# Toeplitz tables from TensorE transposes instead of a store and reload, in an S5 diffusion layer

## The chip, the cores and the metric

One core of a Trainium2 chip runs the kernel. The metric is the device time of one execution in microseconds (us), the median of several runs. Engines: PE (TensorE), DVE (VectorE), ACT (ScalarE), POOL (GpSimd), SP (SyncE, which here issues every DMA).

## The reference, cut to what matters

One layer over 256 latent tokens with 256 context tokens, width 2048. The token mixer is an S5 state space with 128 groups of 16 channels and 64 complex states, in two directions. Then come a gated linear unit (GLU) and a squared-ReLU MLP of width 8192, all in float32.

```python
def s5_scan(u, lam_bar, b_bar, s0, reverse):
    bu = jnp.einsum('btgh,gph->btgp', u, b_bar)
    ...
    _, states = lax.associative_scan(_lin_rec_combine, (a, bu), axis=1, reverse=reverse)
    return states
...
    y_lat = u_lat * d
    for direction in range(2):
        ...
        st_ctx = s5_scan(uc_ctx, lam_bar, b_bar, s0, reverse)
        s_ctx_final = st_ctx[:, 0] if reverse else st_ctx[:, -1]
        st_lat = s5_scan(uc_lat, lam_bar, b_bar, s_ctx_final, reverse)
        y_lat = y_lat + jnp.einsum('btgp,ghp->btgh', st_lat, c_mat).real
    ...
        z = jax.nn.gelu(y.reshape(h.shape).astype(h.dtype))
        a, g = jnp.split(z @ w_glu, 2, axis=-1)
        return a * jax.nn.sigmoid(g)
```

`h_lat` is `x` after an RMS norm, a scale and a shift that come from `silu(c) @ w_mod`. The MLP is `jnp.square(jax.nn.relu(h @ w1)) @ w2`.

## The kernel before, in words

**Chunks.** The 256 tokens of a stream are 32 chunks of 8 (`L`). Within a chunk the state space is a fixed linear map from 8x16 inputs to 8x16 outputs per group (a block Toeplitz table with the skip `d` on its diagonal); between chunks only the state is carried. The 128 groups are 16 blocks of 8 (`NB`), and the blocks make three scan units of 4, 6 and 6 (`UNITS`).

**Work of a block b**, each half `hf` being four groups:

1. `xn_blk` and `u_blk` (L565 to L576) normalise and modulate the inputs in place, three operations of 512 columns. POOL does them, but for the modulation of the first two blocks, which is DVE's.
2. `e_sums` (L590, POOL) makes sums of the powers `Qr`, `Qi` and of the matrices `B`. `e_op` (L604, DVE) makes the table `e` with five operations of 512 columns for each half.
3. `e_tr` (L619, PE) transposes `e`, `e_ev` (ACT) copies it out as `et`, `v_mm` (L697, PE) multiplies it with the inputs, and `v_ev` (ACT) puts the results into the unit's scan arrays `ctx` and `lat`.
4. `strip` (L631, PE) multiplies `e` with the block-diagonal matrix `cbd` of `C`, which `c_diag` (ACT) fills. That gives the first block column of the Toeplitz table for both directions. `strip_ev` (ACT) copies it to `sk`. For each pair of blocks `b2`, `w_tr` (L645, PE) transposes it, `w_ev` (ACT) lays it out as one strip `W` of 15 shifts, `dd_mul` (POOL) makes the skip and `w_diag` (L671, DVE) adds it.
5. `w_out` (L676, SP) stores the strip in DRAM, and `load_it` (L685, SP) reads it back with eight DMAs of 128 KB, each at another shift, so that the table `it` stands in SBUF with its rows in place. `it` has one buffer; for the pairs 5 and 7 a second one in another pool.

**Scan of a unit** (`step_op`, L719, DVE): five doubling levels over the context chunks, then 31 steps over the latent chunks of three dependent operations each.

**Output of a block.** `d_sums` (L746, POOL) and `d_op` (L759, DVE, six operations of 512 columns) make the table of `C` times powers, in the ring `dx` of four half-block buffers. `sp_copy` (ACT) and `sp_sum` (L782, POOL) lay out the states. `out_mm` (L785, PE) sums `it` times the inputs and three products of table and states; `gelu` (ACT) and `z_tr` (L806, DVE, a transpose in 32x32 blocks) follow for each pair.

**Weights** come as items of 1 MB in the ring `raw` of three buffers (`RAWBUFS`), in the order in which they are used: 32 of `w_mod` for the scale and shift of the mixer (`a_mm`, L467), 32 for the gates (`k_mm`, L478), and the GLU's. The first ten GLU items are multiplied as they are (`g_mm`, L991), as soon as the gelu outputs that they need exist; the other 22 are split into two parts first (`w_hi`, `w_lo`, then three products at L998) and wait until the whole S5 stage is closed (`close_s5`). After the GLU come the second norm and the MLP (L1325 and L1358), whose loops are written out after the plan.

**The order** of all this is made by `Plan` (L47): a list scheduler that takes each task with its engine, a length in us written in the code, its priority, the tasks before it and the buffers (rings) that it takes and gives back. It emits the tasks in that order, so each engine's queue, and SP's with its DMAs, is a fixed sequence. A task that waits holds up all that stands behind it on its engine. An instruction of POOL or DVE is recorded under L122 where the helper `tt` issued it.

Of the kernel before, what the change touches and what calls it, by code (L numbers as in the profile page):

```python
# [8 lines left out]
F32 = mybir.dt.float32  # L9
# [18 lines left out]
RAWBUFS = 3  # L28
# [11 lines left out]
UNITS = (4, 6, 6)  # L40
PI = math.pi
# [75 lines left out]
def _body(ctx, tc, nc, I, O):  # L117
# [111 lines left out]
    with psx:  # L229
# [15 lines left out]
        m16 = sb.tile([64, H], F32, name="m16")  # L245
        dcol = sb.tile([64, 32], F32, name="dcol")
# [34 lines left out]
        for dst, src in ((m16, "m16"), (dcol, "dcol"), (bcol, "bcol"), (sel4, "sel4")):  # L281
            S.dma_start(dst, I[src])
        V.memset(cst, 0.0)
        V.memset(epst, EPS)
        sk = ew.tile([128, L, 4, H], F32, name="sk")
        cbd = [ew.tile([128, 8, 2, 32], F32, name=f"cbd{n}") for n in range(2)]
        for t in cbd:
            GP.memset(t, 0.0)
# [42 lines left out]
        cm = {V: tmp("c0", [128, NB, 4, 8]), GP: tmp("c1", [128, NB, 4, 8])}  # L331
# [31 lines left out]
        cmul(GP, at(p_, 2), at(p_, 0), at(p_, 1))  # L363
        cmul(GP, span(p_, 4, 8), span(p_, 0, 4), rept(p_, 3, 4))
# [38 lines left out]
        for name, cap in (("ada", 1), ("ev", 1), ("bcb", 2), ("bcs", 2), ("bcc", 2), ("s1e", 2), ("s2e", 1), ("sd", 2), ("cbd", 2),  # L403
                          ("k1", 1), ("dd", 1), ("e", 2), ("et", 2), ("tr", 2), ("st", 1), ("v", 1), ("x", 2), ("yv", 1), ("sk", 1), ("W", 1), ("it", 1),
                          ("ctx", 1), ("lat", 2), ("dx", 4), ("sp", 2), ("z", 1), ("t", 1), ("it2", 1)):
            plan.ring(name, [0.0] * cap)
        plan.ring("raw", [])
        for n in "bsc":
            plan.rings["bc" + n][1].clear()
# [4 lines left out]
        PR = dict(ada=4, T=20, st=3, V=1, W=5, om=5, E=0, D=2, D0=8, gate=0, k4=5, gap=1, p=-1, ars=3, g=6, g2=20, evm=10, eg1=6, x1=6, zlo=4, z=8, ada2=0, k4l=4, acc=20, lo=1, hi=5, sums='Pool', spsum='Pool')  # L414
# [26 lines left out]
        def close_pre():  # L441
            nonlocal lp_, wk, drp
# [3 lines left out]
            drp = p1.enter_context(tc.tile_pool(name="drp", bufs=1, space=bass.MemoryType.DRAM))  # L446

        lp_ = wk = drp = None
        qt = [add("ACT", 0.85, lambda d=d, s=s, l=l: q_copy(d, s, l, 2, NB), prio=1) for d, s in ((Qr, qr), (Qi, qi)) for l in (True, False)]
        pt = [add("ACT", 0.95, lambda d=d, s=s, g=g, l=l: p_copy(d, s, g, l), prio=PR["p"]) for d, s, g in ((Pr, pr, 1.0), (Pn, pi, -1.0)) for l in (True, False)]  # L450
        t = []
# [10 lines left out]
        for n in range(RB, min(nq + RB, len(items))):  # L462
            rawt[n] = add("SP", 2.91, lambda n=n: load_to(n + 1), prio=2, take=("raw",), lag=1.3)
# [74 lines left out]
        for n, key in enumerate(queue):  # L538
# [26 lines left out]
        def xn_blk(b):  # L565
            x = xv[b // BQ][:, :, (b % BQ) * 8:(b % BQ) * 8 + 8]
            tt(GP, x, x, rs.rearrange("p (i c) -> p i c", i=2).unsqueeze(2).to_broadcast([128, 2, 8, C]), ALU.mult)
# [10 lines left out]
        for b in range(NB):  # L578
            t = add("Pool", 1.23, lambda b=b: xn_blk(b), prio=3 + b, ready=28.7)
            on_v = b < 2  # L580
            ut[b] = add("DVE" if on_v else "Pool", 1.33 if on_v else 2.05, lambda b=b, e=V if on_v else GP: u_blk(b, e), [t, vect[chunk_of[b]]],
                        prio=0 if on_v else 2 + b)
# [3 lines left out]
        for b in range(2, NB):  # L586
            for n in "bsc":
                bcl[n, b] = add("SP", 0.45, lambda n=n, b=b: load_bc(n, b), prio=0, take=("bc" + n,), lag=2.0)

        def e_sums(b):  # L590
            Bv = bct.pop(("b", b))
            s1 = ew.tile([128, L, 8], F32, tag="s1e", bufs=2, name="s1e")
# [3 lines left out]
            tt(SE, s2[:, 1], Bv[:, 0], Bv[:, 1], ALU.subtract)  # L596
            est[b] = Bv, s1, s2

        def c_diag(b):
            Cv = bct.pop(("s", b))  # L600
            act(cbd[b % 2][0:64, :, :, 0:H], Cv[0:64].rearrange("p r g h -> p g r h"))
            act(cbd[b % 2][64:128, :, :, H:], Cv[64:128].rearrange("p r g h -> p g r h"))

        def e_op(b, hf, k):  # L604

# [3 lines left out]
            if k == 0:  # L609
                est[b, hf] = (ew.tile([128, 4, L, H], F32, tag="k1e", bufs=1, name="k1"),  # L610
                              ew.tile([128, 2, 4, L, H], F32, tag="e", bufs=2, name="e"))
            k1, e = est[b, hf]
            if k < 3:
                o, p, c = ((k1, s1, Bv[:, 0]), (e[:, 1], Qr[:, b], s2[:, 0]), (e[:, 0], Qi[:, b], s2[:, 1]))[k]
                tt(V, o, p[:, :, hs].rearrange("p t g -> p g t").unsqueeze(3).to_broadcast(n), c[:, hs].unsqueeze(2).to_broadcast(n), ALU.mult)
            else:
                tt(V, e[:, k - 3], k1, e[:, k - 3], ALU.subtract)

        def e_tr(b, hf, r):  # L619
            e = est[b, hf][1]  # L620
            est["ps"] = pst("tr", 2)
            for gi in range(4):
                PE.transpose(est["ps"][:, gi * 128:(gi + 1) * 128], e[:, r, gi].rearrange("p s h -> p (s h)"), ident)  # L623
# [6 lines left out]

        def strip(b, hf):  # L631
            e = est[b, hf][1]
            est["st", b, hf] = st = pst("st", 1)
            for r in range(2):
                for j in range(4):
                    PE.matmul(st[32 * j:32 * j + 32, :128], cbd[b % 2][:, hf * 4 + j, r], e[:, r, j].rearrange("p s h -> p (s h)"),
                              start=(r == 0), stop=(r == 1))

        def strip_ev(b, hf):
            lp = 2 * (b % 2) + hf  # L640
            act(sk[:, :, lp], est.pop(("st", b, hf))[:, :128].rearrange("p (s h) -> p s h", h=H))
# [839 lines left out]
```

## Time and profile before

| what | us |
|---|---|
| median of 3 runs (1309.31 to 1315.62) | 1313.72 |
| the profiled execution's own time | 1313.43 |
| its span, first to last instruction | 1311.7 |
| PE busy | 1178.7 |
| DVE busy | 897.1 |
| ACT busy | 539.4 |
| POOL busy | 192.5 |

The span is 1.7 us short of the execution's time, which is 0.3 us below the median. Busy time is the union of an engine's recorded instructions; for PE their ends are modelled. In the rows further on, a line of the timeline or of a group of instructions reads: start, duration, engine, line, operation, output<-inputs, shape, count; groups give the busy time and the mean in ns of one, then the idle time before them.

### The profile page before, as it was taken

How to read it: one execution, taken by the hardware profiler on the slowest of the kernel's cores; microseconds unless marked ns; L12 is line 12 of the kernel's file. 1: busy time of each engine (PE TensorE's matmuls, PEld its weight loads, DVE VectorE, ACT ScalarE, POOL GpSimd, SP SyncE). 2: the span in 40 equal slices, each digit the busy share in tenths (PEclk: the TensorE clock that was granted, in tenths of full speed). 3: DMA queues.
4: the chain of work that ended last, by engine and by line, in shares of the span. 5: the costliest groups of instructions: out<-in, count | busy, mean ns of one | idle time of the engine just before them, and what ended most of it. 6: DMA issues, size and time to landing. Idle time of an engine off the chain costs nothing.

```text
span 1311.7 us, 22524 instructions
## 1 busy us (share of the span) xinstructions
PE 1178.7 (90%) x9457; PEld 957.2 (73%) x9457; DVE 897.1 (68%) x1200; ACT 539.4 (41%) x731; POOL 192.5 (15%) x200
## 2 busy tenths in 40 slices
PE   4576884696898999989999999999999999999997
PEld 1454553452434688989999999999978888888885
DVE  8999999878878677765555565555655555655555
ACT  5442544242115534574333334333434444444443
POOL 4766344611322000030000000000000000000000
PEclk8588997798899999999999999999999999999998
DMA  7488868989986888816656666566656555555552
GB/s 269 148 213 295 316 245 195 307 307 196 260 227 168 319 346 324 317 66 224 234 219 245 217 220 250 209 242 223 230 189 224 192 193 184 182 185 188 192 192 97
DMA packets 74093, 296.68 MB, mean 226 GB/s; under 512 B 7164, under 2 KB 30588, under 8 KB 48520
## 3 DMA queue, kind: packets, MB, share of 16 engines
q1 hardware_dynamic: 73992, 295.25, 66.3%
q8 instruction: 74, 1.21, 0.4%
q14 instruction: 27, 0.22, 0.1%
HBM read 291.15 MB, written 4.07 MB: 225 GB/s over the span
## 4 chain that ended last, share of the span: by engine, by line
PE 74%; DMA 9%; DVE 5%; SPq 1%; ACT 1%; issue 1%; POOL 0%; DVEq 0%; POOLq 0%; ACTq 0%
PE m L1325 27%; PE o L1358 27%; PE gb L998 9%; DMA raw<-wk 4%; PE gb L991 3%; DMA it<-wd 2%; DMA raw<-wa 2%; DVE e L122 2%; SPq L689 1%; PE ada L484 1%; PE y L800 1%; PE v L706 1%; DMA bcc<-bc 1%; PE m L1247 1%; PE ada L476 1%
## 5 line engine op out<-in xcount | busy, mean ns | idle before, releaser
L122 DVE TENSOR_TENSOR wlo<-raw,whi 128x2048 fp32r<-128x2048 f32 x126 | 288.7, 2291 | 134.7 <-ACT whi L125 134.7
L1325 PE MATMUL m<-h,whi 128*128 128x256 f32 x1984 | 248.2, 283 | 0.0
L125 ACT ACTIVATE whi<-raw 128x2048 fp32r<-128x2048 f32 (+1 forms) x130 | 243.8, 1876 | 1.5 <-PE m L1247 1.5
L1325 PEld LDWEIGHTS m<-h,whi 128*128 128x128 f32 x1984 | 242.5, 192 | 0.0
L1358 PE MATMUL o<-wlo,hh 128*128 128x512 f32 x512 | 160.5, 395 | 0.2 <-DVE wlo L122 0.2
L1358 PE MATMUL o<-whi,hh 128*128 128x512 f32 x512 | 160.6, 395 | 0.0
L1358 PE MATMUL o<-whi,hl 128*128 128x512 f32 x512 | 160.5, 395 | 0.0
L1325 PE MATMUL m<-h,wlo 128*128 128x256 f32 x992 | 129.1, 283 | 0.0
L1325 PEld LDWEIGHTS m<-h,wlo 128*128 128x128 f32 x992 | 123.5, 192 | 0.0
L125 ACT ACTIVATE hh<-hid 128x512 fp32r<-128x512 f32 x64 | 40.5, 633 | 194.5 <-PE o L1358 194.5
L125 ACT ACTIVATE r<-m 128x256 f32<-128x256 f32 x64 | 24.6, 384 | 222.9 <-PE m L1325 221.1
L1358 PEld LDWEIGHTS o<-wlo,hh 128*128 128x128 f32 x512 | 95.9, 187 | 24.1 <-DVE wlo L122 0.6
L1358 PEld LDWEIGHTS o<-whi,hh 128*128 128x128 f32 x512 | 95.8, 187 | 24.2 <-ACT hh L125 0.8
L1358 PEld LDWEIGHTS o<-whi,hl 128*128 128x128 f32 x512 | 96.0, 187 | 23.5
L1297 DVE TENSOR_TENSOR hl<-hid,hh 128x512 fp32r<-128x512 f32 x64 | 44.3, 693 | 88.8 <-ACT hh L125 88.7
L1269 DVE TENSOR_TENSOR hid<-r,m 128x256 f32<-128x256 f32 x64 | 26.9, 421 | 91.9 <-ACT r L125 91.9
L991 PE MATMUL gb<-raw,xz 128*128 128x512 f32 x160 | 76.0, 623 | 2.4 <-DMA raw<-wg 2.3
L623 PE MATMUL tr<-ident,e 128*128 128x128 f32 x256 | 44.7, 315 | 30.9 <-DVE e L122 24.6
L998 PE MATMUL gb<-hi,zs 128*128 128x512 f32 (+1 forms) x288 | 70.1, 357 | 0.0
L484 PE MATMUL ada<-raw,cst 128*32 128x512 f32 x256 | 36.9, 654 | 35.4 <-DMA raw<-wk 35.4
L623 PEld LDWEIGHTS tr<-ident,e 128*128 128x128 f32 x256 | 32.5, 160 | 45.8 <-DVE e L122 21.4
L991 PEld LDWEIGHTS gb<-raw,xz 128*128 128x128 f32 x160 | 30.2, 197 | 46.5 <-issue 40.2
(202 smaller groups left out, 1613.2 us busy)
## 6 DMA issues: line engine op xcount, KB each, us to landing
raw<-w SPq DMA_DIRECT2D x128, 1024.0 KB, 4.8
raw<-wk SPq DMA_DIRECT2D x48, 1024.0 KB, 8.4
raw<-wa SPq DMA_DIRECT2D x32, 1024.0 KB, 7.4
raw<-wg SPq DMA_DIRECT2D x32, 1024.0 KB, 5.2
k<-wk SPq DMA_DIRECT2D x16, 1024.0 KB, 7.3
it<-wd SPq DMA_DIRECT2D x64, 128.0 KB, 6.9
xz<-xs SPq DMA_DIRECT2D x4, 1024.0 KB, 9.1
bcb<-bc SPq DMA_DIRECT2D x16, 128.0 KB, 8.9
```

The source lines that it names most:

```text
L122: eng.tensor_tensor(out=out, in0=a, in1=b, op=op)
L125: A.activation(out=out, in_=in_, func=f, **kw)
L476: PE.matmul(adab["a"][32 * j:32 * j + 32, :n], cst[:, 2 * kt:2 * kt + 32], w[:, e, j], start=(kt == 0), stop=(kt == KT - 1))
L484: PE.matmul(adab["k"][32 * j:32 * j + 32, :], cst[:, 2 * kt:2 * kt + 32], w[:, j * 512:(j + 1) * 512], start=(kt == k0), stop=(kt == KT - ...
L623: PE.transpose(est["ps"][:, gi * 128:(gi + 1) * 128], e[:, r, gi].rearrange("p s h -> p (s h)"), ident)
L689: S.dma_start(it[16 * s:16 * s + 16], wdt[b2][:, :, (7 - s) * H:(7 - s) * H + 128])
L991: PE.matmul(banks[p][nk * t + k], xz[kt // BQ][:, GQ * C + (kt % BQ) * T + t * 128:][:, :128], wt[:, (nk * e + k) * 512:(nk * e + k + 1) * ...
L998: PE.matmul(banks[p][nk * t + k][:, :wd], a, w[:, (nk * e + k) * wd:(nk * e + k + 1) * wd], start=ff, stop=ll)
L1269: V.tensor_tensor(out=hid[:, nt], in0=r, in1=ps, op=ALU.mult)
L1297: V.tensor_tensor(out=hl, in0=hid[:, 2 * i:2 * i + 2], in1=hh.bitcast(F32), op=ALU.subtract)
L1325: PE.matmul(ps, w[a][:, kt], (h2h, h2l)[b][:, kt], start=a == b == kt == 0, stop=a == 1 and kt == KT - 1)
L1358: PE.matmul(banks[nh][2 * t + k], w[2 + x][:, e, zz], w[y][:, e * 1024 + k * 512:e * 1024 + k * 512 + 512], start=f and n == 0 and e == es ...
```

## The change: what it does

- The skip enters through PE: `dg_op` (ACT) scales the identity by the column `d` of the block, and one matmul of 240 columns with the constant `dsel` opens the accumulation in `strip`.
- `strip` now writes both directions side by side into one 15-shift strip of a PSUM bank, for both halves: 32 instead of 16 products of each block's table (8 to 16 for each half; each is two PE instructions). `cz`, a table with zeros around `C`, takes the place of `cbd`.
- `ext_ev` (ACT) copies the strip out once for each block. `t_tr` (PE) transposes eight shifted windows of it, in two groups of four, and `t_ev` (ACT) copies them out as `it`, in SBUF. `yl_mm` multiplies `it` with the inputs at once, and `yl_ev` (ACT) stores the result over the latent inputs.
- `out_mm` loses its products with `it` and adds the stored result through one matmul of 256 columns with the identity.
- Gone are `strip_ev`, `w_tr`, `w_ev`, `dd_mul`, `w_diag`, `w_out` and `load_it`, with their rings.
- DVE takes over from POOL: `xn_blk`, `u_blk`, `e_sums`, `d_sums`, `sp_sum` and two complex products of the opening. POOL keeps its memsets and the subtraction `h2_lo` after the GLU.
- `z_tr` reads PSUM and comes before `gelu`, which works in place.
- `RAWBUFS` is 4; the ring `dx` has three buffers for four, `k1` two for one, `hf` two for four.
- The C matrices for the strip come from a second copy in DRAM with another layout, `cs`.
- Many lengths in the plan are other numbers (a transpose group of `e` 0.52 for 0.43, `strip` 1.0 for 0.57, `out_mm` 1.9 for 2.35, `sp_copy` 2.25 for 1.04, a weight load 3.2 for 2.91), so that the order of the queues is another one.

The core of the diff:

```diff
-RAWBUFS = 3
+RAWBUFS = 4
...
-        cmul(GP, at(p_, 2), at(p_, 0), at(p_, 1))
-        cmul(GP, span(p_, 4, 8), span(p_, 0, 4), rept(p_, 3, 4))
+        cmul(V, at(p_, 2), at(p_, 0), at(p_, 1))
...
+        pw = add("DVE", 4.0, lambda: cmul(V, span(p_, 4, 8), span(p_, 0, 4), rept(p_, 3, 4)), prio=PR["pw"])
...
-            tt(GP, x, x, rs.rearrange(...), ALU.mult)
+            tt(V, x, x, rs.rearrange(...), ALU.mult)
...
-            tt(SE, s1, Qr[:, b], Qi[:, b], ALU.add)
+            V.scalar_tensor_tensor(out=s1, in0=Qr[:, b], scalar=-1.0, in1=Qi[:, b], op0=ALU.mult, op1=ALU.subtract)
...
         def strip(b, hf):
-            e = est[b, hf][1]
-            est["st", b, hf] = st = pst("st", 1)
-            for r in range(2):
+            k1, e = est[b, hf]
+            if hf == 0:
+                est["st", b] = pst("st", 1)
+                PE.matmul(est["st", b][:, :15 * H], est["dg"], dsel.rearrange("p s h -> p (s h)"), start=True, stop=False)
+            st = est["st", b]
+            for n, (r, w) in enumerate(((0, e[:, 0]), (1, e[:, 1]), (2, k1))[:3 if (b, hf) in PE_SUMS else 2]):
+                for d in range(2):
+                    for j in range(4):
+                        PE.matmul(st[32 * j:32 * j + 32, 7 * H * d:7 * H * d + 128], cz[:, d, r, j, hf * H:hf * H + 32], w[:, j].rearrange("p s h -> p (s h)"),
+                                  start=False, stop=(...))
+        def ext_ev(b):
+            est["x1", b] = x = ew.tile([128, 15 * H], F32, tag="x1", bufs=2, name="x1")
+            act(x, est.pop(("st", b))[:, :15 * H], scale=-1.0)
+
+        def t_tr(b, th):
+            est["tp", b, th] = ps = pst("st", 1, "tp")
+            for i in range(4):
+                t = 4 * th + i
+                PE.transpose(ps[:, i * 128:(i + 1) * 128], est["x1", b][:, (7 - t) * H:(7 - t) * H + 128], ident)
...
+        def yl_mm(b):
+            est["yl", b] = ps = pst("st", 1, "yl")
+            yv = ps[:, :256].rearrange("p (t e h) -> p t e h", e=2, h=H)
+            for e in range(2):
                 for j in range(4):
+                    gi = 2 * j + e
+                    PE.matmul(yv[32 * j:32 * j + 32, :, e, :], xv[b // BQ][:, 0, (b % BQ) * 8 + gi], est["it", b][:, :, 2 * (gi % 4) + gi // 4, :], start=True, stop=True)
...
-        def w_out(b2):
-            wdt[b2] = wd = drp.tile([H, 16, 240], F32, tag="wd", bufs=8, name="wd")
-            S.dma_start(wd.rearrange("h (l j) f -> l h (j f)", l=4), wst[b2].rearrange("p j t h -> p (j t h)"))
-        def load_it(b2):
-            r = it_ring(b2)
-            itab[b2] = it = (lp_ if r == "it" else tail["whl"]).tile([128, 16, 128], F32, tag=r, bufs=1, name="it")
-            for s in range(L):
-                S.dma_start(it[16 * s:16 * s + 16], wdt[b2][:, :, (7 - s) * H:(7 - s) * H + 128])
...
         def out_mm(b):
+            PE.matmul(yb[b2][:, 256 * w:256 * w + 256], ident, xv[b // BQ][:, 0, (b % BQ) * 8:(b % BQ) * 8 + 8].rearrange("p g c -> p (g c)"), start=True, stop=False)
             for e in range(2):
-                for f, k in ((None, None), (0, 2), (1, 0), (2, 1)):
+                for f, k in ((0, 2), (1, 0), (2, 1)):
```

## Rows read from the trace of the kernel before

**Rows 1.** Busy time by stretch; instructions, granted PE clock, DMA share, GB/s.

```profile
0.00:40.00 40.00, 15.43 (x169) 7.60 (x170) 33.87 (x72) 24.20 (x40) 19.27 (x27) 0.77 0.73 273
40.00:291.00 251.00, 181.57 (x2950) 122.98 (x2948) 234.82 (x482) 100.03 (x237) 128.97 (x119) 0.85 0.79 251
291.00:388.00 97.00, 75.76 (x576) 35.45 (x574) 80.02 (x198) 18.14 (x23) 20.99 (x24) 0.91 0.97 239
388.00:436.00 48.00, 42.63 (x449) 21.24 (x447) 33.71 (x45) 25.80 (x32) 11.01 (x13) 1.00 0.66 187
436.00:574.00 138.00, 134.75 (x707) 113.76 (x706) 102.83 (x101) 67.09 (x112) 1.90 (x3) 0.99 0.77 297
574.00:1311.70 737.70, 728.61 (x4615) 656.16 (x4614) 411.80 (x305) 304.16 (x291) 10.35 (x15) 1.00 0.56 203
```

Its columns are the stretch, its length, then busy us with the number of instructions of PE, PE's weight loads, DVE, ACT and POOL, and the three named last.

**Rows 2.** The chain that ended last, from the page, by line.

```profile
PE m L1325 27%; PE o L1358 27%; PE gb L998 9%; DMA raw<-wk 4%; PE gb L991 3%; DMA it<-wd 2%; DMA raw<-wa 2%; DVE e L122 2%; SPq L689 1%; PE ada L484 1%; PE y L800 1%; PE v L706 1%; DMA bcc<-bc 1%; PE m L1247 1%; PE ada L476 1%
```

**Rows 3.** Timeline of POOL and DVE, around 218 us and around 284 us.

```profile
217.80 1.14 POOL L122 TENSOR_TENSOR sp<-sp 128x256 f32<-128x256 f32 x1 [3.01 <-ACT sp L125]
224.12 14.41 POOL L122 TENSOR_TENSOR s1e<-Qr,Qi 128x64 f32<-128x64 f32 x1
...
218.27 1.22 DVE L122 TENSOR_TENSOR e<-Qr,s2e 128x512 f32<-128x512 f32 x1
...
283.40 0.68 DVE L122 TENSOR_TENSOR e<-Qr,s2e 128x512 f32<-128x512 f32 x1
284.00 0.35 DVE L727 TENSOR_TENSOR t<-ARS,lat 128x192 f32<-128x192 f32 x1
```

**Rows 4.** Groups of DVE instructions by shape, 0 to 436 us.

```profile
L122 DVE TENSOR_TENSOR e<-k,e 128x512 f32<-128x512 f32 x64 | 48.4, 763 | 0.1
L122 DVE TENSOR_TENSOR e<-Qi,s2e 128x512 f32<-128x512 f32 x32 | 26.2, 818 | 0.0
L122 DVE TENSOR_TENSOR k<-s1e,bcb 128x512 f32<-128x512 f32 x32 | 24.8, 774 | 2.3 <-POOL s1e L122 2.3
L727 DVE TENSOR_TENSOR t<-ARS,lat 128x128 f32<-128x128 f32 x31 | 14.0, 453 | 0.3
L734 DVE TENSOR_TENSOR lat<-lat,t 128x64 f32<-128x64 f32 x31 | 11.7, 376 | 0.4
L372 DVE TENSOR_TENSOR t<-li,aim 128x128 f32<-128x128 f32 x1 | 1.4, 1358 | 0.0
L367 DVE TENSOR_TENSOR den<-are 128x128 f32<-128x128 f32 x1 | 1.3, 1284 | 0.0
```

**Rows 5.** The same view: shapes that ran without POOL beside them.

```profile
L374 DVE TENSOR_TENSOR qr<-t,den 128x128 f32<-128x128 f32 x1 | 0.3, 292 | 0.0
L122 DVE TENSOR_TENSOR qr<-qr,c 128x256 f32<-128x256 f32 x1 | 0.4, 426 | 0.0
L732 DVE TENSOR_TENSOR ctx<-ctx,t 128x64 f32<-128x64 f32 x1 | 0.2, 225 | 0.0
```

**Rows 6.** Timeline of SP: two of the reloads, each of eight DMAs.

```profile
295.22 12.41 SPq L689 DMA_DIRECT2D it<-wd  x8
...
394.37 5.92 SPq L689 DMA_DIRECT2D it<-wd  x8
```

**Rows 7.** Groups of PE matmuls by shape, 0 to 436 us.

```profile
L991 PE MATMUL gb<-raw,xz 128*128 128x512 f32 x160 | 76.0, 623 | 2.4 <-DMA raw<-wg 2.3
L636 PE MATMUL st<-e,cbd 128*32 128x128 f32 x512 | 22.5, 298 | 0.9 <-DVE W L673 0.5 <-ACT sk L125 0.4
L798 PE MATMUL y<-it,xz 128*32 128x128 f32 x256 | 15.9, 307 | 5.9 <-DMA bcc<-bc 4.5 <-ACT z L125 1.4
L649 PE MATMUL wps<-ident,sk 128*64 128x128 f32 x64 | 10.8, 296 | 0.8 <-ACT W L125 0.8
```

**Rows 8.** The chain that ended last, in order of time: `v_mm` at both clocks.

```profile
261.61 1.91 PE v L706 x32
...
265.75 1.08 PE v L706 x32
```

More of the change, by code (lines that the diff above doesn't have):

```diff
@@ L40 @@
 UNITS = (4, 6, 6)
+PE_SUMS = ()
 PI = math.pi
@@ L284, in _body @@
         V.memset(epst, EPS)
[L285 to L288, printed above, removed]
+        cz = ew.tile([128, 2, 3, 4, 3 * H], F32, name="cz")
+        GP.memset(cz, 0.0)
         def tmp(name, shape=None):
@@ L445, in close_pre @@
             wk = p1.enter_context(tc.tile_pool(name="wk", bufs=1))
[L446 to L451, printed above, removed]
+        lp_ = wk = None
+        qt = [add("ACT", 0.97, lambda d=d, s=s, l=l: q_copy(d, s, l, 2, NB), prio=1) for d, s in ((Qr, qr), (Qi, qi)) for l in (True, False)]
+        pw = add("DVE", 4.0, lambda: cmul(V, span(p_, 4, 8), span(p_, 0, 4), rept(p_, 3, 4)), prio=PR["pw"])
+        pt = [add("ACT", 1.07, lambda d=d, s=s, g=g, l=l: p_copy(d, s, g, l), [pw], prio=PR["p"]) for d, s, g in ((Pr, pr, 1.0), (Pn, pi, -1.0)) for l in (True, False)]
+        t = [pw]
         for m in range(5):
@@ L462, in _body @@
         for n in range(RB, min(nq + RB, len(items))):
-            rawt[n] = add("SP", 2.91, lambda n=n: load_to(n + 1), prio=2, take=("raw",), lag=1.3)
+            rawt[n] = add("SP", 3.2, lambda n=n: load_to(n + 1), prio=2, take=("raw",), lag=2.0)
         adab = {}
@@ L578, in _body @@
         for b in range(NB):
[L579 to L582, printed above, removed]
+            t = add("DVE", 0.61, lambda b=b: xn_blk(b), prio=PR["xn"])
+            ut[b] = add("DVE", 1.33, lambda b=b: u_blk(b, V), [t, vect[chunk_of[b]]], prio=PR["u"])
         est, ett, bcl = {}, {}, {}
@@ L815, in _body @@
             on_v = PR["sums"] == "DVE"
-            esum = add(PR["sums"], 0.55 if on_v else 1.1, lambda b=b: e_sums(b), ([bcl["b", b]] if b > 1 else []) + gate + (qt if b == 2 else []), prio=1, take=("s1e", "s2e"))
-            cb = add("ACT", 0.6, lambda b=b: c_diag(b), [bcl["s", b]] if b > 1 else [], prio=1, take=("cbd",), give=("bcs",))
+            esum = add(PR["sums"], 0.42 if on_v else 1.1, lambda b=b: e_sums(b), ([bcl["b", b]] if b > 1 else []) + gate + (qt if b == 2 else []), prio=1, take=("s1e", "s2e"))
+            cs = [bcl["s", b]] if b > 1 else []
+            if sums(b):
+                cs = [add("DVE", 0.2, lambda b=b: c_sum(b), cs, prio=1)]
+            cb = add("ACT", 1.05 if sums(b) else 0.84, lambda b=b: c_diag(b), cs, prio=1, take=("cz",), give=("bcs",))
+            dg = add("ACT", 0.28, lambda b=b: dg_op(b), prio=1, take=("dg",))
             for hf in range(2):
@@ L825, in _body @@
+                if not pe:
+                    o.append(add("DVE", 0.6, lambda b=b, h=hf: e_op(b, h, 3), [(o[0], 0.13), (o[1], 0.13), (o[2], 0.0)], prio=p))
+                    o.append(add("DVE", 0.6, lambda b=b, h=hf: e_op(b, h, 4), [(o[3], 0.0), (o[2], 0.13)], prio=p, give=("k1",)))
                 tps, evs = [], []
                 for r in range(2):
[L827 to L828 removed]
+                    tps.append(add("PE", 0.97 if pe else 0.52, lambda b=b, h=hf, r=r: e_tr(b, h, r), [o[1 + r] if pe else o[3 + r]] + tps, prio=PR["T"], take=("tr",)))
+                    evs.append(add("ACT", 0.5, lambda b=b, h=hf, r=r: e_ev(b, h, r), [tps[r]] + [(x, 0.0) for x in evs], prio=0,
@@ L835, in _body @@
+                vm = add("PE", 1.08, lambda b=b, h=hf: v_mm(b, h), [evs[1], ut[b]] + ([evt["vm"]] if "vm" in evt else []), prio=PR["V"], take=("v",), give=("et",))
                 evt["vm"] = vm
@@ L882, in _body @@
         swp = virt(swap, etasks)
-        for b2, wo in itw.items():
-            itt[b2] = add("SP", 4.72, lambda b2=b2: load_it(b2), [wo, swp], prio=1, take=("it2",), lag=2.0)
         for b in range(NB):
```

204 lines of the change are left out of this document (91 added, 113 removed).

## The prediction

> **What bounds the kernel now.** I first cut the span into stretches [rows 1]. The last two, the split part of the GLU (436 to 574 us) and the MLP (574 to the end), are 138 + 737.7 = 875.7 us, and PE is busy for 134.75 and 728.61 of them. Nothing of the change lies there but a fourth weight buffer and the ring of `hf`, so I carry them over unchanged. All that can move is the 436 us before. There the bound differs from stretch to stretch. From 40 to 291 us, the E stage (tables, strips, scans of the first two units), DVE is busy for 234.82 of 251 us, PE for 181.57 at a mean granted clock of 0.85, and POOL for 128.97. From 291 to 388 us the third scan runs, and DVE has only 80.02 of 97 us. From 388 to 436 us PE does the last outputs and leftover early GLU products, 42.63 of 48 us.
>
> Next the chain of waits [rows 2]: besides PE it names the landing of `it` from DRAM (2%) and SP issuing those loads at L689 (1%), about 39 us of the span together. The queue of SP shows how [rows 6]: the eight DMAs of one reload hold SP for 5.92 us at best and 12.41 at worst, and behind them wait the weight loads and the C loads.
>
> Last the timeline, for what POOL does to DVE [rows 3]. A DVE operation of 512 columns is recorded with 0.68 us and the next starts 0.60 later. At 218.27, with `sp_sum` of POOL running since 217.80, the same operation took 1.22. POOL suffers too: its sum of 64 columns at 224.12 lasted 14.41 us beside a dense DVE. So two-input work on both engines delays both.
>
> **The change part by part.**
>
> *DVE regains what POOL cost it.* In the groups [rows 4] against the undisturbed lengths [rows 3, 5]: 64 x (763 - 680) = 5.3 us, 32 x (818 - 680) = 4.4, 32 x (774 - 680) = 3.0, the first unit's steps 31 x (453 - 292) = 5.0 and 31 x (376 - 225) = 4.7. That is 22 us in 190 instructions. The E stage has 482 DVE instructions [rows 1]; at the same loss for each it would be 57. I take 40, since the counted groups hold the longest operations of the stage; the ends are 22 and 57. In the opening, five operations from L367 to L373 took 1.28 to 1.36 us for 0.29 [rows 4, 5]: 5 us, in some 6.6 us of time. POOL is busy for 19.27 of the first 40 us [rows 1]; at the same loss beside all of it, 19.27 x 5 / 6.6 = 15. I take 11, nearer that end, since the rest of POOL's time (`xn_blk`) lies beside the first products of E; ends 5 and 15.
>
> *DVE takes over.* At 0.60 us for 512 columns [rows 3], about 0.34 for 256 and 0.20 for 128 (the lengths 0.43 and 0.29 of [rows 5], less the 0.08 by which neighbours overlap): `xn_blk` 16 x 0.60 = 9.6; `u_blk` 28 x 0.60 = 16.8; `e_sums` 16 x (0.20 + 0.20 + 0.13) = 8.5; the large complex product 6 x 0.60 = 3.6; `d_sums` another 8.5, of which some 2.6 fall into the E stage; `sp_sum` 16 x 0.34 = 5.4, of which 1.4. In the E stage 42.5 us, in all 53. The small complex product adds 6 x 0.20 = 1.2 to the opening. `w_diag` goes: 16 small adds of 0.22 [rows 5], 3.6 us.
>
> The Trainium skill (GPSIMD Engine Reference, 3.1 Elementwise — side-by-side cycle accounting) puts a two-input add on GpSimd at 1.96 times VectorE's time. Applied to POOL's busy time before 436 us [rows 1], 180 us, that would be an estimated 92 us for DVE, and the sum would come to about 1313. The trace speaks against it: POOL's time holds its own waiting (the 14.41 us above), while DVE's lengths for these very shapes are in the rows.
>
> E stage, DVE: 234.8 - 40 + 42.5 - 3.6 = 234 us. **Moving POOL's work is thus a draw in that stage**, and its end comes earlier only by the opening, 11 - 1.2, or 10 us. DVE's 16 idle us stay as they are.
>
> *PE in the E stage.* The strips cost 22.5 us for 512 instructions [rows 7]; twice the count adds 22.5. The transposes go from 64 to 128 instructions, adding 10.8. The products with `it` (15.9) move from `out_mm` to the E stage for three quarters of the blocks, 12. The matmul with `dsel` and the one with the identity: 76.0 / 160 = 0.48 us for an instruction of 512 columns, so about 0.48 for one matmul of 240 or 256 columns in two instructions; 16 of each, 7.7 + 7.7, of which 10 in the stage. That is 55 us by busy records, whose ends are modelled; the same calls follow each other faster at full clock, for `v_mm` 1.08 against 1.91 us [rows 8], so the low end is 55 / 1.77 = 31. Of the stage's 241 us PE would then need 181.6 + 31 to 55: 213 to 237. That is close to full. What eases it is the clock: at 0.85 some 30% of the stage runs at the lower of the two levels (1.2 for 2.4 GHz), and at the higher one 181.6 would be 181.6 x (0.7 + 0.3 / 1.77) = 158 us. I take 195 to 205 of 241, hidden beside DVE, and charge nothing; if that cover is gone, see the second rival.
>
> *ACT.* It gets a few more copies for each block, on an engine with 100 of 251 us busy [rows 1]. The new chain strip, copy, transposes, copy, product, copy runs through one PSUM bank (`st`), about ten handoffs for each block. Its users are queued on PE and ACT in the plan's order; DVE waits for it only through the buffers of `e`. Charged at nothing, since a block has about 15 us (251 / 16).
>
> *The reload goes.* In 291 to 388 us DVE idles for 17 of 97 us, from late `dx` buffers, which `out_mm` holds while it waits for `it`. New work there is 6 us of sums, less some 3 of contention. With DVE at 0.95 of the stretch: (80 + 3) / 0.95 = 87, a gain of 10; ends 0 (the scan's dependent steps stay) and 17. The weight loads no longer stand behind up to 12.41 us of reload, and have a fourth buffer. Late next is PE: early GLU products and outputs.
>
> *The end of S5.* After the third scan 48 us pass [rows 1], PE busy for 42.63. Outputs of six blocks and the last three of the ten early items (16 instructions of 0.48 each, 23 us) remain. The last reload's 5.92 us go; I take 5, ends 0 and 10. `z_tr` before `gelu` is the same chain.
>
> *The order by other lengths* can win part of the 16 us that DVE idles in the E stage, or lose some. I take 7; ends -10 and 16.
>
> *`hf` with two buffers* and the later stages: POOL works there one after another anyway; 0, at most 1 us lost.
>
> **Sum:** 10 + 10 + 5 + 7 = 32 us off the profiled execution's 1313.4, which stands 0.3 below the median: 1281.
>
> **The rivals.**
>
> 1. *Only one of the two gains arrives.* If the end of S5 is set by weight loads and early GLU products (160 instructions, 76.0 us [rows 7]) rather than by the reload, the last three terms shrink and about 12 us are left: 1301. For it: PE's 42.63 of 48 us. Against: the reload is in the chain by name [rows 2].
>
> 2. *PE becomes the bound of the E stage: slower.* The place is the E stage's queue on PE, where transposes and strips for the tables stand ahead of the products that feed the scan. If PE's idle 69 us of that stage are handoffs that nothing fills, the stage grows by what PE gets more, 31 to 55 us, say 45. Less the 10 of the opening, the 10 and 5 of later and 2 of the order that is +18: 1331. It decides from the point where PE has over 0.9 of the stage, 217 us, within my 213 to 237 for an unchanged clock. Against: the clock rises with denser work, and 0.85 leaves room.
>
> 3. *The moved work costs DVE more than its clean rows.* Its operands are broadcast and strided in other ways than the shapes of [rows 5]. The nearest row above is POOL's own busy time, 180 us; half of it, 90, is 37 more than 53, and 32 of that in the E and scan stages gives 1313, no change. Against: the products of E are broadcast too and keep 0.68 us [rows 3].
>
> 4. *More:* DVE regains 56 instead of 40, the order closes DVE's gaps, and PE's clock rises: another 17 + 8 us, 1256. That the tables might still come from DRAM is excluded by the diff.
>
> **How the numbers follow.** Chances: forecast 0.54, its own range 1267 to 1296 (the ends of reload, end of S5 and order, not all at once); rival 1 0.18; rival 2 0.11; rival 3 0.07; rival 4 0.10. A range of 1255 to 1310 leaves out rival 2, half of rival 3 and half of rival 4, 0.2 together. A measurement of this kernel can tell a change of about 0.5%, 6.6 us, from none. Faster by more: 0.54 + 0.18 + 0.10, less 0.01 of rival 1's upper end: 0.81. Within: 0.07 of rival 3 and that 0.01: 0.08. Slower: 0.11.
>
> **What would show it.** Right: DVE operations of 512 columns all at 0.68; E stage's last `e` at about 281 us (291 before), the third scan's end at about 368 (388), the first L998 at about 404 (436), and the rest 875 us as before. DVE busy in the E stage about 234 us, PE 195 to 205 at a clock above 0.85. Wrong: PE near full in the E stage with DVE waiting for `st` or `et` (rival 2); waits of L991 for `raw` before the first L998 (rival 1); DVE busy time far above 234 without POOL (rival 3).

## The result, and the profile after

The changed kernel takes **1291.7 us** (median of four runs, 1290.6 to 1292.0) against 1314.6 for the kernel before beside it; the ratio of the two is 0.983, with a 95% interval of 0.981 to 0.986. The prediction was 1281 us, range 1255 to 1310: the sign is right, and the time is 10.7 us above the point forecast. The profiled execution took 1291.92 us, with a span of 1290.1.

The stretches of [rows 1] now look like this. The columns are the same; the cuts are at the same events as far as the trace shows them, with a sixth stretch of its own between the end of the GLU and the MLP's loop:

```profile
0.00:40.00 40.00, 19.04 (x296) 10.33 (x296) 33.60 (x98) 22.38 (x41) 1.26 (x5) 0.83 0.87 325
40.00:281.00 241.00, 212.07 (x3667) 144.94 (x3668) 225.88 (x595) 117.20 (x254) 0.00 (x0) 0.94 0.72 273
281.00:357.00 76.00, 65.72 (x461) 31.73 (x459) 72.76 (x195) 19.77 (x22) 0.00 (x0) 0.96 0.43 149
357.00:405.80 48.80, 40.89 (x353) 21.57 (x353) 33.15 (x60) 24.12 (x29) 0.95 (x1) 0.85 0.46 160
405.80:530.30 124.50, 124.50 (x631) 103.89 (x634) 88.90 (x71) 53.80 (x73) 0.00 (x0) 1.00 0.80 304
530.30:564.30 34.00, 23.27 (x177) 21.68 (x170) 22.86 (x44) 22.79 (x60) 11.52 (x16) 0.85 0.17 63
564.30:1290.10 725.80, 717.01 (x4521) 644.65 (x4519) 403.91 (x292) 295.45 (x270) 0.95 (x1) 1.00 0.58 205
```

The stretch from the GLU's end to the MLP's loop in the kernel before, by the same view, for comparison:

```profile
559.30:585.90 26.60, 23.13 (x178) 21.77 (x179) 16.56 (x36) 20.24 (x56) 11.29 (x16) 0.94 0.05 20
```

Up to the start of the late (split) GLU the change won 30.2 us: 405.8 against 436.0. The late GLU lasts 124.4 us (123.3 before), and from the MLP's loop to the last product both kernels take 717.3. But the stretch between those two grew from 26.4 to 34.0 us. So 8.7 of the 30.2 us were given back after the changed part of the code: 1.1 in the late GLU, 7.6 behind it.

The DVE groups, up to 405.8 us, answer to [rows 4]. The 512-column products are at 0.68 us, 64-column scan steps at 0.22 for 0.376, and the 128-wide product at 0.287 for 0.453:

```profile
L124 DVE TENSOR_TENSOR e<-k,e 128x512 f32<-128x512 f32 x64 | 42.7, 682 | 0.0
L124 DVE TENSOR_TENSOR e<-Qi,s2e 128x512 f32<-128x512 f32 x32 | 21.9, 683 | 9.8 <-PE st L661 9.8
L728 DVE TENSOR_TENSOR t<-ARS,lat 128x128 f32<-128x128 f32 x31 | 8.9, 287 | 0.5
L735 DVE TENSOR_TENSOR lat<-lat,t 128x64 f32<-128x64 f32 x31 | 6.8, 220 | 0.5
```

The PE groups, up to 405.8 us, answer to [rows 7]. The strips' matmuls doubled in number, and `tp` and `yl` (transposes and products with `it`) are new places of old work:

```profile
L985 PE MATMUL gb<-raw,xz 128*128 128x512 f32 x160 | 72.5, 601 | 0.0
L661 PE MATMUL st<-e,cz 128*32 128x128 f32 x1024 | 34.4, 275 | 0.0
L673 PE MATMUL tp<-ident,x 128*128 128x128 f32 x128 | 20.7, 284 | 2.6 <-ACT it L127 1.6 <-ACT x L127 1.0
L687 PE MATMUL yl<-it,xz 128*32 128x128 f32 x256 | 11.1, 295 | 1.0 <-ACT it L127 1.0
```

Where the 8.7 us went is seen in DVE's timeline around the end of the late GLU at 530.2:

```profile
526.14 2.35 DVE L207 SCALAR_TENSOR_TENSOR acc<-k,cst,acc 128x2048 f32<-128x2048 f32 x1 [6.43 <-DMA k<-wk]
...
530.65 1.22 DVE L966 TENSOR_TENSOR wlo<-raw,whi 128x1024 fp32r<-128x1024 f32 x1
...
534.25 1.21 DVE L966 TENSOR_TENSOR wlo<-raw,whi 128x1024 fp32r<-128x1024 f32 x1
...
536.40 4.06 DVE L1157 SCALAR_TENSOR_TENSOR xn<-yg,rsd,xn 128x512 f32<-128x512 f32 x6
...
541.95 0.29 DVE L1152 TENSOR_SCALAR dg<-ident,rsd 128x128 f32<-128x128 f32 x1
```

DVE stands 6.43 us before 526.14, until the last load `k<-wk` lands. Then come the four `wlo` splits of the first W1 blocks, and only from 536.40 the `xn` operations of the second norm, whose end lets the `hp` products start at 542.30, 12.1 us after the GLU (4.9 before). In the kernel before, the same last addition and the first and last of the four splits lie ahead of the late GLU's end at 559.3:

```profile
546.46 2.35 DVE L205 SCALAR_TENSOR_TENSOR acc<-k,cst,acc 128x2048 f32<-128x2048 f32 x1
548.72 1.22 DVE L972 TENSOR_TENSOR wlo<-raw,whi 128x1024 fp32r<-128x1024 f32 x1
...
555.16 1.22 DVE L972 TENSOR_TENSOR wlo<-raw,whi 128x1024 fp32r<-128x1024 f32 x1 [0.44 <-ACT whi L125]
```

The reader has to know what `acc<-k` is, since the change does not touch it. The scale of the second norm comes from a part of `w_mod` that is not multiplied on PE: 16 loads of 1 MB (`k4_load`) go through the two buffers `xz0` and `xz1`, and DVE adds each, weighted, to `acc` (`acc_op`, 2.35 us). The loads can start only when S5 is closed and `z` is split, for the same buffers held the inputs until then; and the splits of the first W1 blocks write into these buffers, so they wait for the last addition. Call it the **k chain**. It took 123 to 124 us in both kernels, from its first load (424.8 before, 405.2 after) to the end of its last addition (548.8 and 528.5). Before, it ended 10.5 us ahead of the late GLU's end; after, 1.7 us ahead. The first k loads in the queue of SP, before and then after:

```profile
424.81 0.38 SPq L1056 DMA_DIRECT2D k<-wk  x1
...
405.19 11.19 SPq L1050 DMA_DIRECT2D k<-wk  x3
```

That is the theory with which the experiments were made from the fifth on; the first four were made while the delay was still put down to other things.

### The profile page after: what moved, and what is told of

Read it like the earlier page. It is cut to its first block, busy times and chain, and to the rows that moved or that the text cites. A ratio compares the mean times of both kernels' runs of the same rounds, so it can differ in the third digit from the quotient of the medians.

```text
span 1290.1 us, 23542 instructions
## 1 busy us (share of the span) xinstructions
PE 1202.5 (93%) x10097; PEld 978.8 (76%) x10097; DVE 881.1 (68%) x1352; ACT 555.5 (43%) x747; POOL 14.7 (1%) x23
## 4 chain that ended last, share of the span: by engine, by line
PE 73%; DVE 21%; ACT 2%; DMA 1%; issue 1%; POOL 0%; DVEq 0%; SPq 0%; ACTq 0%
PE m L1319 28%; PE o L1352 27%; PE gb L992 10%; DVE e L124 4%; DVE dx L124 2%; PE gb L985 2%; DVE t L728 2%; DVE xz L124 2%; DVE t L731 1%; DMA raw<-wa 1%; DVE lat L735 1%; DVE lat L733 1%; PE ada L482 1%; PE y L799 1%; DVE k L124 1%
## 5 line engine op out<-in xcount | busy, mean ns | idle before, releaser
L985 PE MATMUL gb<-raw,xz 128*128 128x512 f32 x160 | 72.5, 601 | 0.0
L992 PE MATMUL gb<-hi,zs 128*128 128x512 f32 (+1 forms) x288 | 71.0, 357 | 0.0
L992 PE MATMUL gb<-lo,zs 128*128 128x512 f32 (+1 forms) x208 | 61.2, 360 | 0.0
L992 PEld LDWEIGHTS gb<-hi,zs 128*128 128x128 f32 x288 | 49.8, 188 | 10.2 <-issue 1.5
L985 PEld LDWEIGHTS gb<-raw,xz 128*128 128x128 f32 x160 | 29.2, 190 | 35.0 <-issue 35.0
L127 ACT ACTIVATE hi<-raw 128x1024 fp32r<-128x1024 f32 x30 | 30.4, 1053 | 49.3 <-PE gb L992 28.9
```

What stands on the lines that cost most here:

```text
L127: A.activation(out=out, in_=in_, func=f, **kw)
L985: PE.matmul(banks[p][nk * t + k], xz[kt // BQ][:, GQ * C + (kt % BQ) * T + t * 128:][:, :128], wt[:, (nk * e + k) * 512:(nk * e + k + 1) * ...
L992: PE.matmul(banks[p][nk * t + k][:, :wd], a, w[:, (nk * e + k) * wd:(nk * e + k + 1) * wd], start=ff, stop=ll)
```

## The experiments

All times are medians; the other columns are read from the one profiled execution of each run. "margin" is how far the last k addition ends ahead of the late GLU's end, "transition" the time from that end to the MLP's loop.

| kernel | time | last `e` | scan end | late GLU | margin | transition |
|---|---|---|---|---|---|---|
| before | 1312 to 1315 | 286.5 | 386.9 | 436.0 to 559.3 | 10.5 | 26.4 |
| after | 1291.7 | 276.1 | 356.5 | 405.8 to 530.2 | 1.7 | 34.0 |
| e1 | 1299.6 | 275.2 | 355.6 | 405.7 to 530.2 | -12.0 | 42.6 |
| e2 | 1299.5 | 272.2 | 359.3 | 403.2 to 530.2 | -0.7 | 44.5 |
| e3 | 1302.5 | 281.4 | 357.6 | 407.7 to 531.3 | -0.5 | 42.9 |
| e4 | 1302.1 | 286.0 | 373.4 | 421.0 to 544.6 | 8.4 | 31.4 |
| e5 | 1282.0 | 275.8 | 356.3 | 405.3 to 529.7 | 16.6 | 26.8 |
| e6 | 1312.0 | 287.1 | 385.6 | 434.9 to 558.2 | 36.7 | 26.6 |
| e7 | 1300.2 | 294.0 | 370.6 | 419.5 to 545.6 | 16.6 | 27.0 |
| e8 | 1284.1 | 270.2 | 358.4 | 402.3 to 529.3 | 28.5 | 27.3 |
| e9 | 1321.7 | 313.3 | 393.7 | 443.8 to 568.3 | 16.6 | 27.2 |
| e10 | 1289.3 | 278.8 | 360.5 | 410.2 to 534.6 | 16.6 | 26.5 |

From the MLP's loop to the last product every one of them takes 717.3 us.

**e1: another planned length for the late GLU's products.**

```diff
-                    dur, dep, give = nk * 0.693, ...
+                    dur, dep, give = nk * 0.64, ...
```

> The changed kernel with one number of the plan put back: 0.64 instead of 0.693 us for a late GLU product, so only the order can differ. Theory (the 8.6 us lost after 406 us come from an order that puts the four splits of the MLP's first weights, 4.9 us of DVE, ahead of the second norm, because the plan thinks PE later than it is): the stretch from the last late product to the MLP's loop falls from 34.0 to about 27 us and the time to about 1285. Rival (the last loads of the scale weights come late, 6.4 us of DVE's wait, whatever the order; or the two buffers of hf): the time stays within 2 us of 1291.7.

1299.6 us, ratio to before 0.989 (0.985 to 0.994). Both expectations missed: the time is 7.9 us above the changed kernel's. The GLU did not move, but the transition grew to 42.6. The queue of SP shows why, with four k loads behind the loads of W1, and PE's timeline what it costs:

```profile
517.20 13.61 SPq L1050 DMA_DIRECT2D k<-wk  x4
```

```profile
538.60 5.62 PE L1168 MATMUL hp<-dg,xn 128*128 128x128 f32 x28 [8.44 <-DVE dg L1152]
544.14 1.06 PE L1134 MATMUL ada<-acc,ones 128*32 128x512 f32 x8
...
548.37 0.95 PE L538 MATMUL cp<-sel,evg 128*128 128x4 f32 x8
```

The products that turn `acc` into the scale (L1134, L538) come after the first `hp`, and the 32 copies to `h` wait for them. This run made the k chain the suspect.

**e2 and e3: three weight buffers; the same with four `dx` buffers.**

```diff
-RAWBUFS = 4
+RAWBUFS = 3
```

```diff
-... ("lat", 2), ("dx", 3), ...
+... ("lat", 2), ("dx", 4), ...
-                    dtab[b, hf] = wk.tile([128, 3, L, 4, H], F32, tag="dx", bufs=3, name="dx")
+                    dtab[b, hf] = wk.tile([128, 3, L, 4, H], F32, tag="dx", bufs=4, name="dx")
```

> The changed kernel with three weight buffers instead of four. Theory (weights did not bound the E stage, whose DMA share is near nothing from 260 to 280 us with all buffers full): 1289 to 1296. Rival (the fourth buffer, not the gone reload, lets the weights run ahead, and brought a good part of the 30 us gained before the late GLU): 1300 or more.

> As the one before, and the ring of output tables (dx) has four buffers again. Theory (five half tables are left for DVE after the third scan, while DVE runs the last 15 steps of that scan with nothing between them): 3 to 5 us under the run with three weight buffers, and fewer dx operations after the scan's end. Rival (PE's early GLU products set the end of S5 anyway): within 1 us of it.

1299.5 and 1302.5 us, ratios 0.990 (0.986 to 0.994) and 0.993 (0.990 to 0.995). The theories of both missed: e2 is 3.5 us above its range and half a us short of its rival's 1300, and e3 is 3 us above e2 instead of below. In e2 the late GLU ends at 530.2, exactly as after, so the fourth buffer had won nothing up to there; all of the loss is in the transition, 44.5 us, where the margin is gone (-0.7). The margin alone does not give the transition's length, for e1 with -12.0 has 42.6. e8 repeats e2 with the k chain out of the way.

**e4: the kernel before without store and reload.** The eight loads of `it` and `w_out` are left out, and the products run on one tile of zeros; what the Toeplitz tables add to the output is missing.

```diff
-                wo = add("SP", 0.68, lambda b2=b2: w_out(b2), ...)
-                ...  itt[b2] = add("SP", 4.72, lambda b2=b2: load_it(b2), ...)
+                add("X", 0.0, lambda: None, [(wg, wg["lag"])], give=("W",), lag=0.0)
...
-            sp, it = spt.pop(b), itab[b2]
+            sp, it = spt.pop(b), itab[0]
```

> The kernel before, its strip computed but not stored, and the table not loaded: out_mm multiplies with a tile of zeros, so the Toeplitz part of the output is left out. Theory (the prediction's terms for the reload and the end of S5, 10 + 5 us): 1296 to 1302. Rival A (the reload is hidden, weights and PE set those stretches): 1310 to 1316. Rival B (the reload is the whole of the gain, and moving POOL's work brought nothing): 1283 to 1288.

1302.1 us, ratio 0.992 (0.989 to 0.995), 0.1 above the theory's range and 8 or more from both rivals'. The late GLU starts 14.9 us earlier (421.0): 13.5 of it are there when the third scan ends, 0.5 when the last `e` does. Here too 5 us are given back in the transition, with a margin of 8.4 instead of 10.5. So the reload is worth about 15 of the 30.2 us by itself.

**e5: the k chain first.**

```diff
-        PR = dict(..., k4l=4, acc=20, ...)
+        PR = dict(..., k4l=1, acc=-1, ...)
...
-            ld = add("SP", 3.3, lambda kt=kt: k4_load(kt), ..., take=(ring,), lag=1.3)
+            ld = add("SP", 3.3, lambda kt=kt: k4_load(kt), ..., take=(ring,), lag=5.0)
```

> The changed kernel with one edit in the plan: the 16 loads of the block k behind the second norm's scale are ranked before the weight loads, their additions before other DVE work, and their planned landing is 5.0 us after issue instead of 1.3. SP's planned order then alternates one k and one weight load and ends the k loads before the last two weight blocks. Theory (the gain was given back because the k chain, 123 us long in both kernels, ends 1.8 us before the last late GLU product instead of 10.6, and the scale and the first W1 splits wait for it): the last addition ends 15 us or more before the end of the late GLU, the hp products start 4 to 6 us after it instead of 12.1, the stretch from the late GLU's end to the MLP's loop goes from 34.0 to about 27, and the time is 1284 to 1287 against 1291.7. Rival (the stretch is long because of the DVE's queue order or the lower clock there, not because of the k chain): it stays above 32 and the time within 2 us of 1291.7. Second rival (the alternating loads starve the late GLU): late GLU above 127 us instead of 124.4 and no gain.

**1282.0 us**, ratio 0.978 (0.975 to 0.980), the fastest of the study, 9.7 us below the changed kernel (8.3 by the profiled executions) and 2 below the theory's range. Up to the late GLU hardly anything moved (405.3 for 405.8), its length stayed 124.5, and the transition fell to 26.8. DVE's and PE's timelines:

```profile
510.80 2.35 DVE L207 SCALAR_TENSOR_TENSOR acc<-k,cst,acc 128x2048 f32<-128x2048 f32 x1
...
518.21 3.49 DVE L966 TENSOR_TENSOR wlo<-raw,whi 128x1024 fp32r<-128x1024 f32 x3
```

```profile
531.46 1.05 PE L538 MATMUL cp<-sel,evg 128*128 128x4 f32 x8 [0.72 <-ACT evg L127]
534.61 9.28 PE L1168 MATMUL hp<-dg,xn 128*128 128x128 f32 x64 [2.10 <-DVE dg L1152]
```

The splits of W1 now run beside the late GLU, and `hp` starts 4.9 us after it, as before the change. The edit touches nothing but the rank and the planned landing of the k chain, so what DVE's queue order and the lower clock (0.85 there, 0.94 in e5) cost in that stretch came from this chain: the cause is shown.

**e6: the same edit in the kernel before.**

> The same edit of the plan in the kernel before. Theory (there the k chain ended 10.6 us ahead of the late GLU's end and cost nothing): the time stays within 4 us of the kernel before run beside it, the stretch to the MLP's loop within 2 of 26.4. Rival (the k chain cost both kernels the same): faster by 6 us or more.

1312.0 us, ratio 0.9998 (0.998 to 1.002): nothing, though the margin rose from 10.5 to 36.7. Here a margin of 10.5 us is enough, and more buys nothing (e4, with 8.4, gave back 5).

**e7: e5 with the elementwise work back on GpSimd.** Scaling and projection of the first norm (but for two blocks' projection) and the sums of both stages, as they were before; the two complex products of the opening stay on DVE, and the tables still come from transposes.

```diff
-        PR = dict(..., sums='DVE', spsum='DVE')
+        PR = dict(..., sums='Pool', spsum='Pool')
...
-            t = add("DVE", 0.61, lambda b=b: xn_blk(b), ...)
-            ut[b] = add("DVE", 1.33, lambda b=b: u_blk(b, V), ...)
+            t = add("Pool", 1.23, lambda b=b: xn_blk(b), prio=3 + b, ready=28.7)
+            ut[b] = add("DVE" if on_v else "Pool", ..., lambda b=b, e=V if on_v else GP: u_blk(b, e), ...)
```

> e5 with the elementwise work back on GpSimd as in the kernel before (first norm's scaling and projection of all but two blocks, the sums of both stages, the sum for the outputs); the tables still come from transposes. Theory of the prediction (taking that work over is a draw for DVE in the E stage; the gain of the third scan is mostly the reload): the last e at 270 to 283 us (276.1 in the changed kernel), DVE's 512-column operations at 0.76 to 0.82 us instead of 0.68, start of the late GLU at 402 to 414 (405.8), time within 8 us of e5. Rival A (freeing DVE of GpSimd's contention made most of the gain): last e at 286 or later, late GLU at 416 or later, time 10 us or more above e5. Rival B (GpSimd was free extra capacity and giving it up cost time): last e before 268, late GLU before 400, time 6 us or more below e5.

1300.2 us, 18.3 above e5 (16.1 by the profiled executions); ratio 0.992 (0.989 to 0.994). Rival A is right and the prediction's theory of a draw is not: the last `e` is 18.1 us later, the late GLU 14.2. Up to the last `e`, by stretch, e5 and then e7:

```profile
0.00:275.80 275.80, 225.72 (x3859) 151.84 (x3859) 254.74 (x677) 136.76 (x289) 1.26 (x5) 0.93 0.75 286
```

```profile
0.00:294.00 294.00, 234.96 (x3825) 156.65 (x3825) 271.90 (x584) 138.62 (x284) 129.24 (x123) 0.91 0.74 274
```

e7 has 93 DVE instructions fewer there and is busy 17.2 us longer. With each instruction counted from its start to the start of the next, or to its own end if that comes first, the work that e5 does on DVE and e7 does not is 41.1 us in that stretch (`u_blk` 18.1, `xn_blk` 9.6, the sums 13.4). Less some 7 us of scan and output operations that e7 does earlier, GpSimd's work cost DVE 17.2 + 41.1 - 7, or about 51 us.

**e8: e5 with three weight buffers** (`RAWBUFS = 3` as in e2).

> e5 with three weight buffers instead of four. Theory (the fourth buffer bought nothing; what three buffers lost in the earlier run was the k chain at the end): start of the late GLU at 403 to 406, stretch from its end to the MLP's loop 27, time within 3 us of e5's 1282.0. Rival (the fourth buffer carries a part of the gain): 1286 or more, with the late GLU starting later or lasting above 128 us.

1284.1 us, ratio 0.979 (0.976 to 0.981): 2.1 above e5, within the theory. The late GLU starts 3.0 earlier, 0.7 before the theory's range, and lasts 2.5 longer. The fourth buffer is worth nothing up to the GLU's end, and the loss of e2 was the k chain.

**e9: work on GpSimd that nobody waits for.**

```diff
+        scr = sb.tile([128, 512], F32, name="scr")
+        GP.memset(scr, 0.0)
...
+                for w in (512, 128, 128) if hf == 0 else (512, 512, 128):
+                    add("Pool", 1.2 if w == 512 else 0.5, lambda w=w: tt(GP, scr[:, :w], scr[:, :w], scr[:, :w], ALU.add), [o[0]])
```

> e5 with work on GpSimd that nobody waits for: in every block of the E stage three additions of 512 columns and three of 128 on a scratch tile of its own, 96 in all, about as many as the moved work had there. The outputs' computation is unchanged. Theory (e7 was 18 us slower because operations on GpSimd slow DVE's, not because DVE waits for their results): DVE's 512-column operations at 0.72 to 0.82 us, the scan's steps lengthened most, the last e 20 us or more after e5's 275.8, time 15 us or more above e5's 1282.0. Rival (e7 lost by waits and order): DVE's operations keep 0.68, the last e within 5 us of 275.8, time within 4 us of e5.

1321.7 us, ratio to before 1.007 (1.004 to 1.010), 39.7 above e5: the theory's sign and size, but not its place. The plan gave each addition a place beside a block, yet no data hold GpSimd back, so it ran all 96 in one go from the start, and the loss is in the opening and the first blocks, where 36 DVE operations of 512 columns (first norm and first tables) took 1.08 us on average (0.68 in e5); the scan's steps kept their length. GpSimd's timeline, and e9 up to its last `e`, against e5's row above:

```profile
2.30 95.38 POOL L124 TENSOR_TENSOR scr<-scr 128x512 f32<-128x512 f32 x96
```

```profile
0.00:313.30 313.30, 224.94 (x3859) 152.07 (x3859) 296.98 (x677) 136.48 (x289) 89.65 (x102) 0.89 0.67 252
```

The same 677 DVE instructions, in the same order, take 296.98 us for 254.74: 42 us for 88 us of GpSimd (89.65 less the 1.6 of its memsets), with no value passed between the two. All of it is lost while GpSimd works. The first 139 DVE instructions and the rest up to the last `e`, in e5 and then in e9:

```profile
0.00:57.50 57.50, 33.29 (x541) 22.34 (x542) 49.58 (x139) 28.56 (x49) 1.26 (x5) 0.76 0.84 317
57.50:275.80 218.30, 192.43 (x3320) 129.50 (x3318) 205.16 (x539) 108.20 (x240) 0.00 (x0) 0.97 0.73 278
```

```profile
0.00:98.10 98.10, 34.87 (x585) 24.27 (x588) 91.85 (x139) 29.92 (x53) 89.65 (x102) 0.70 0.52 191
98.10:313.30 215.20, 190.07 (x3280) 127.80 (x3272) 205.13 (x539) 106.56 (x236) 0.00 (x0) 0.97 0.74 279
```

The groups of the first 46 us show single operations on 128 columns that are 0.29 us undisturbed [rows 5], and in e5 (0.284 and 0.291):

```profile
L124 DVE TENSOR_TENSOR c<-qi,pi 128x128 f32<-128x128 f32 x1 | 1.1, 1123 | 0.0
L379 DVE TENSOR_TENSOR t<-t,t 128x128 f32<-128x128 f32 x1 | 1.0, 1011 | 0.0
```

**e10: the transposes of the tables twice.**

```diff
+                for _ in range(2):
                     PE.transpose(ps[:, i * 128:(i + 1) * 128], est["x1", b][:, (7 - t) * H:(7 - t) * H + 128], ident)
```

> e5 with the 128 transposes that build the Toeplitz tables done twice, about 19 us more of PE work in the E stage (120 of them take 19.5 us busy there), over 230 of its 235 us in all. Theory (DVE sets the E stage and PE's added work is hidden): the last e within 4 us of 275.8, time within 4 us of e5's 1282.0. Rival (PE already sets the pace at places; DVE waits 9.8 us there for the strips): the last e 8 to 20 us later, time 6 us or more above e5.

1289.3 us, 7.3 above e5; ratio 0.982 (0.979 to 0.985). Neither expectation fits whole: the last `e` is only 2.9 us later, as the theory had it, but the late GLU is 4.9 later and the time 7 above, as the rival had it. Part of PE's work in the E stage is thus paid. PE in that stretch, against 225.72 in e5's row:

```profile
0.00:278.80 278.80, 234.13 (x3975) 163.54 (x3975) 255.21 (x677) 136.73 (x288) 1.26 (x5) 0.94 0.75 283
```

The runs spread over 6 us, so how much of it is paid is open: 4.6 us by the profiled executions' spans (1281.9 and 1286.5), 7.3 by the medians.

## Why the prediction was right and wrong

**The sum up to the late GLU** was 32 us off, and 30.2 came; the first L992 is at 405.8 for the forecast 404. The terms under it were less right than their sum, and that they add up to nearly the forecast is luck: the opening and the order, put at 17, brought about 1 by the count below, and taking work off GpSimd behind the opening, put at nothing, brought 14.2.

- *Opening and the end of E, forecast 10:* the last `e` is 10.4 earlier. But the opening won 5.1, not 10 (the first operation after the reciprocal of the norm starts at 26.61 for 31.71), and the E stage won the rest, with 32 scan operations more done by then.
- *"Moving POOL's work is thus a draw in that stage":* wrong in size. Contention was put at 40 us and measured at about 51 by e7 (from the start to the last `e`, so with a part of the opening), inside the ends 22 to 57. DVE's taking over was put at 42.5; without the 3.6 of the large complex product, which e7 leaves on DVE, that is 38.9, and 41.1 was measured. The two differ by about 10 us in DVE's favour, where the step had 2.5 against it. By e5 and e7 taking the work off GpSimd is worth 14.2 us at the late GLU.
- *The reload, forecast 10, and the end of S5, forecast 5:* together 14.9 by e4, as forecast, but 13.5 before the scan's end and 1.4 behind it. The text took 5.92 us for a reload's shortest hold of SP; the eight reloads of the kernel before took 5.10 to 6.08 us but for the one of 12.41. The scan stage shrank by 20.0 us (from 100.4 to 80.4), beyond the upper end of 17, because scan steps had moved ahead of it and GpSimd was gone from it too.
- *The end of S5* took 49.0 us and takes 49.2, which is rival 1's picture there; its sign, early GLU products waiting for `raw`, is missing (the L985 row has no idle time before it). Late next was PE, as the text said, but PE waits first: 11.6 us for the last unit's states (the row below). After that come the last outputs, which need those states, and 48 early GLU products (22.2 us).
- *The order, forecast 7:* 30.2 less 14.9 and 14.2 leaves 1.1. In this stands the opening too, whose gain e7 keeps (its first operation after the reciprocal starts at 26.94). If those 5 us last to the late GLU, then order, fourth buffer and PE's added work lost some 4 us together; no run takes these apart.

PE of the changed kernel, while the last scan steps run alone:

```profile
347.70:359.30 11.60, 0.01 (x2) 0.01 (x1) 8.63 (x24) 4.63 (x5) 0.00 (x0) 0.65 0.48 162
```

**The step that failed is the last one, "`hf` with two buffers and the later stages: 0, at most 1 us lost".** It took the 875 us behind the S5 stage as one block that starts when PE gets there, since PE is busy nearly throughout. Beside PE ran a chain that did not start earlier by as much: the k chain started 19.6 us earlier (405.2 for 424.8) where the late GLU started 30.2 earlier. Its 10.5 us of margin became 1.7, and 8.7 us were given back. e5 pays them back with an edit of the plan's order and takes 1282.0 us, 1 us from the predicted 1281; e6 shows that the same edit is worth nothing where the margin was there. The other half of the step held: with the chain out of the way in e5 the transition is 26.8 for 26.4, which leaves 0.4 us to `hf`. The trace of before had the chain, but no part of the prediction asked for its margin: the last addition at 546.46 to 548.81, and behind it the splits of W1 up to 556.38, 2.9 us before the GLU's end.

**PE in the E stage** was put at 195 to 205 of 241 us with a clock above 0.85: it is 212.07, with 0.94, just under the 217 from which rival 2 was to decide. The clock rose, as the second rival's "against" had it, and the E stage is still set by DVE. But e10 shows that the cover was thin, and that rival 2 was nearer than its chance says: DVE already waits 9.8 us there for the strips (the `e<-Qi` row).

**The ratio.** From the ratio in the Trainium skill (GPSIMD Engine Reference, 3.1 Elementwise — side-by-side cycle accounting) the prediction had an estimate of 92 us for the moved work, and set it aside for 53 by the rows. The measured 41.1 us (38.9 forecast for the same operations) sides with the rows: GpSimd's recorded time holds its waiting (14.41 us for a sum of 64 columns [rows 3]), so that the ratio cannot be applied to it. The Trainium skill (SBUF — State Buffer, Who interferes with whom) says that a DVE instruction with two inputs in SBUF contends with a GpSimd instruction that reads SBUF, and calls the pair of ports that they share an exclusive lock. e9 agrees in kind: operations of 0.29 us took 1.01 to 1.12. In sum DVE lost 0.48 us for each us that GpSimd worked, so not every operation was caught.

## What to carry to other kernels

A gain that makes one engine's work start earlier is kept only as far as every parallel chain that the next stage waits for starts earlier too: look for what else ends shortly before the join, and write down its margin. Where two engines slow each other, price a move by undisturbed lengths on one side and by the whole loss on the other: 88 us of GpSimd work that no one needed cost DVE 42 us. And after any change of lengths, look at the queue of SP again: an edit that looked harmless (e1) put four loads of a chain that mattered behind loads that did not.

## What was not expected

GpSimd work without consumers runs as early as its queue allows, whatever place the plan gave it, and in the opening it moved the first `e` from 46.3 to 81.1 us. The fourth weight buffer, a part of the change, bought nothing that the runs can tell (e8). And doubling the transposes added 13 us of busy PE time in `tp` (32.6 for 19.5 in the E stage), yet cost only 2.9 us at the last `e`.
